# Sliding 8x8 windows with stride 4: the order of the band-crossing stores, the last units and five loads

## The chip, the core and the metric

The kernel runs on one core of one Trainium2 chip. Times are microseconds (us) of device time. The core has compute engines that copy data within the on-chip memory (DVE, the vector engine; ACT, the scalar engine; POOL, the general engine, which here only issues transfers), SP, which only issues transfers, and 16 DMA engines that move data between the device memory and the 128 partitions of the on-chip memory. "Row" below means 4096 floats, 16 KB, which lie together in one partition and together in the output.

## The reference

The input x has shape (16, 64, 64, 64): batch, channel, height, width, float32. Each 8x8 window at a stride of 4 is copied out, all channels together; there is no arithmetic.

```python
n_h = (h - window_size) // stride + 1      # 15
n_w = (w - window_size) // stride + 1      # 15
result = np.zeros((batch, n_h, n_w, c, window_size, window_size), dtype=np.float32)
for i in range(n_h):
    for j in range(n_w):
        h_start = i * stride
        w_start = j * stride
        result[:, i, j] = x[:, :, h_start:h_start + window_size, w_start:w_start + window_size].copy()
```

The input has 16.8 MB and the output 59.0 MB: 16 x 15 x 15 = 3600 rows.

## The kernel before, in words

**Layout.** The whole input is loaded once, into the tile L. A partition holds one channel half (ch, two halves of 32 channels), one batch (b, 16) and one horizontal band of 16 image rows (q, 4 bands): partition = ch * 64 + b * 4 + q. The batches come in two groups of eight, y = 0 and 1, so a group of one channel half takes 32 partitions.

**Loads (L56 to L58, L106 to L114).** ACT issues one load of 512 KB (L106: 8 channels of the upper channel half, band 0, all batches). Then, for each y and q, SP issues one load for channels 4 to 31 of channel half 0 (`SMALL` = 4; 896 KB), and POOL one of channels 0 to 3 of that half (128 KB) and one for channel half 1 (1024 KB, or 768 KB for q = 0). SP has eight loads, POOL sixteen. Every one of SP's and POOL's loads writes 8 partitions.

**Units.** A unit fills one of four buffers G (128 partitions x one row) by copies from L, and one store sends its rows out. `tile_()` (L169) hands out the buffers in turn; a buffer is free again when its earlier store has landed. A window at band slot s = 0, 1 or 2 (rows 0, 4, 8 of the band) lies inside a band; the one at slot 3 crosses into the next band, so its lower half comes from the next partition, through a stream shuffle (L151). The units are:

- `part(y, j)` (L174), six of them: one batch group, slots 0 and 1 and two columns j, j + 1; copies of 32 partitions on ACT and DVE (L181).
- `unit(j, 0)` (L189, a plain unit), eight of them, j = 6 to 13: slot 0 in partitions 0 to 63, slot 1 in 64 to 127. In each half `fill` (L139) makes one copy with the first of two copy functions (ACT, L148) and one with the second: `dve` for the three early ones, otherwise `shf` (a stream shuffle that moves nothing across, on DVE, L158) or `mix` (8 of 32 channels on ACT, L162, the others by `shf`).
- `unit(j, 2)` (a crossing unit), fifteen of them, j = 0 to 14: slot 2 in one half of the partitions, copied by ACT; slot 3 in the other, by `shf`, `mix` and the shuffles of L151. `turn` (L198), which alternates, says which half has slot 2. With turn 0 slot 2 lies in partitions 0 to 63 and slot 3 in 64 to 127, and the scatter uses the index tile `idx_hi`; with turn 1 it is the other way round, with `idx_lo`. Band 3 has no slot 3 (that would be window row 15 of 15), so the index of its 16 rows, those with q = 3 in the half that has slot 3, is set past the end of the output and they are not written.

POOL sends out these units by indirect scatters of 128 rows (L128), which know the output row of each partition from the index tile.

**Order.** It is the order of the code, written out by hand: three parts for y = 0; three parts for y = 1, each followed by a plain unit; then five times three crossing units and a plain unit. The 29 units use the buffers 0, 1, 2, 3, 0, ...; the last plain unit (j = 13) is the 29th.

**The last two units (L218 to L230).** Column j = 14 still lacks slots 0 and 1. One buffer is skipped (L219). Each of the two is filled in partitions 32 to 95 by four copies of 32 partitions (L227; for each y one on ACT for channel half 0 and one on DVE for channel half 1), and is stored by four transfers (L230), one for each band q, of 16 rows each (256 KB). The four of s = 0 are issued by SP; of s = 1, q = 0 and 2 by SP, 1 and 3 by ACT. At the end of the kernel SP waits for all transfers (shown under L261).

Of the kernel before, what the change touches and what calls it, by code (L numbers as in the profile page):

```python
# [10 lines left out]
def kernel(  # L11
# [7 lines left out]
    nc = tc.nc  # L19
    P = nc.NUM_PARTITIONS  # L20

    B, C, H, W = x.shape
    Bo, NH, NW, Co, WSo, WSo2 = out.shape
    WS = int(window_size)
    ST = int(stride)
# [5 lines left out]
    CH = 2  # L31
    HQ = P // (B * CH)
    CL = C // CH
    RB = H // HQ
    NSLOT = RB // ST
    NWIN = NH * NW
    CFREE = C * WS * WS
    HP = P // CH
    YB = 8
    NY = B // YB  # L40
    QP = YB * HQ
# [7 lines left out]
    L = lpool.tile([P, CL, RB, W], f32)  # L49
# [1 line left out]

    SMALL, HWP = 4, 8

    def load(eng, ch, y, q, c0, c1):  # L56
        p0 = ch * HP + y * QP + q
        eng.dma_start(out=L[p0 : p0 + QP - HQ + 1 : HQ, c0:c1, :, :], in_=x_v[ch, y, q, :, c0:c1, :])  # L58
# [49 lines left out]
    for y in range(NY):  # L108
        for q in range(HQ):
            hw = y * HQ + q < HWP  # L110
            if hw:
                load(nc.sync, 0, y, q, SMALL, CL)
            load(nc.gpsimd, 0, y, q, 0, SMALL if hw else CL)
            load(nc.gpsimd, 1, y, q, EC if q == 0 else 0, CL)  # L114

# [5 lines left out]
    o_q = out.rearrange("b i j c r w -> i j b (c r w)")  # L121

    def free(st):
        tc.declare_no_dep(st.ins, group="stores", reason="each store writes rows of its own")
        tc.add_to_no_dep_group("stores", st.ins)

    def scatter(g, ix, j, s):
        st = nc.gpsimd.indirect_dma_start(  # L128
            out=o_v,
            out_offset=bass.IndirectOffsetOnAxis(ap=ix[:, 0:1], axis=0),  # L130
            in_=g.rearrange("p c r w -> p (c r w)"),
            in_offset=None,
            element_offset=(s * NW + j) * CFREE,
            bounds_check=B * NWIN - 1,
            oob_is_err=False,
        )
        free(st)

    def fill(g, half, s, j, lo, n, copies):  # L139

        d = slice(half * HP + lo, half * HP + lo + n)
        cols = slice(j * ST, j * ST + WS)
        for ch in (half, 1 - half):
            f = slice(ch * HP + lo, ch * HP + lo + n)
            cs = slice(ch * CL, (ch + 1) * CL)
            copy = copies[ch != half]
            if s < NSLOT - 1:
                copy(out=g[d, cs, :, :], in_=L[f, :, s * ST : s * ST + WS, cols])  # L148
            else:
                copy(out=g[d, cs, 0:ST, :], in_=L[f, :, s * ST : RB, cols])  # L150
                nc.vector.stream_shuffle(out=g[d, cs, ST:WS, :], in_=L[f, :, 0:ST, cols], mask=nxt)  # L151

    act, dve = nc.scalar.copy, nc.vector.tensor_copy
# [3 lines left out]
    def shf(out, in_):  # L157
        nc.vector.stream_shuffle(out=out, in_=in_, mask=same)  # L158

    def mix(out, in_):  # L160
        k = out.shape[1] // 4
        act(out=out[:, 0:k], in_=in_[:, 0:k])  # L162
        shf(out=out[:, k:], in_=in_[:, k:])


    EARLY = 3
    at = 0

    def tile_():  # L169
        nonlocal at  # L170
        at += 1
        return G[(at - 1) % NG]

    def part(y, j):  # L174
        g = tile_()
        for d in range(P // QP):
            s, dj = d // NY, d % NY
            cols = slice((j + dj) * ST, (j + dj) * ST + WS)
            for ch in range(CH):
                f = (ch * NY + y) * QP  # L180
                (act if (2 * d + ch) % 3 == 0 else dve)(  # L181
                    out=g[d * QP : (d + 1) * QP, ch * CL : (ch + 1) * CL, :, :],
                    in_=L[f : f + QP, :, s * ST : s * ST + WS, cols],
                )
        scatter(g, (idx_y0, idx_y1)[y], j, 0)

    crossed = 0

    def unit(j, s, fast=False):  # L189
        nonlocal crossed  # L190
        g = tile_()
        if s == 0:
            fill(g, 0, 0, j, 0, HP, (act, dve if fast else shf))
            fill(g, 1, 1, j, 0, HP, (act, dve if fast else mix))
            scatter(g, idx, j, s)
        else:

            turn = crossed % 2  # L198
            crossed += 1
            fill(g, turn, s, j, 0, HP, (act, act))  # L200
            fill(g, 1 - turn, s + 1, j, 0, HP, (shf, mix))
            scatter(g, (idx_hi, idx_lo)[turn], j, s)

    for n in range(EARLY):
        part(0, 2 * n)
    plain = [(j, 0) for j in range(2 * EARLY, NW - 1)]
    cross = [(j, 2) for j in range(NW)]
    for n in range(EARLY):
        part(1, 2 * n)
        unit(*plain.pop(0), fast=True)  # L210
    while plain:
        for w in cross[:3]:
            unit(*w)
        cross = cross[3:]
        unit(*plain.pop(0))


    j = NW - 1  # L218
    tile_()  # L219
    for s in range(2):  # L220
        g = tile_()
        cols = slice(j * ST, j * ST + WS)
        for y in range(NY):
            d = slice(QP + y * QP, QP + (y + 1) * QP)
            for ch, copy in enumerate((act, dve)):
                f = slice(ch * HP + y * QP, ch * HP + (y + 1) * QP)
                copy(out=g[d, ch * CL : (ch + 1) * CL, :, :], in_=L[f, :, s * ST : s * ST + WS, cols])  # L227
        g_q = g.rearrange("p c r w -> p (c r w)")
        for q in range(HQ):
            free((nc.sync, nc.scalar)[s * q % 2].dma_start(out=o_q[q * NSLOT + s, j], in_=g_q[QP + q : QP + q + (B - 1) * HQ + 1 : HQ]))  # L230


# [33 lines left out]
```

## Time and profile before

| | |
|---|---|
| median of 3 runs | 190.38 us (190.26 to 190.56) |
| span of the profiled execution, from the first to the last instruction | 189.0 us |
| busy: DVE, ACT, POOL | 142.5, 139.2, 46.9 us |
| moved by the DMA engines | 75.81 MB, mean 401 GB/s |
| copies of a full 64-partition half on ACT (L148) | 46 of 1896 ns |

The span is what the profile measures of one execution; the time of a run is taken around the whole execution, and the two differ by 1.4 us. The profile gives no other time for its own execution.

How to read it: the windows give, for a stretch of time, its length, the busy time of DVE, ACT and POOL (with the number of instructions), the clock of the unused matrix engine, the mean busy share of the 16 DMA engines and what they moved. A packet is counted in the window in which it starts, so the share of a short window can be a little off, above 1.0 too. In the timeline a line has start, duration, engine, source line, operation, output<-input, count, and in brackets the idle time before it with what ended it. "POOLq", "SPq" and "ACTq" are the instruction queues of engines: the issue of transfers and waits on semaphores.

### The profile page before, as it was taken

What the parts mean: (1) busy time and instruction counts of PE and PEld (TensorE: products, weight loads), DVE (VectorE), ACT (ScalarE), POOL (GpSimd) and SP (SyncE); (2) the same over time, 40 slices, a digit from 0 to 9 for tenths busy, and PEclk for the clock granted to TensorE, in tenths of its full rate; (3) what the DMA queues carried; (4) which work ended last, traced back from release to release, by engine and by line L of the source; (5) the groups of instructions that cost most, each with busy time, mean ns of one, the idle gap of its engine ahead of it and who ended that gap; (6) DMA issues with size and microseconds to landing.
All of it is one profiled execution on the core that took longest, in us unless ns stands there. A gap on an engine that the chain in (4) does not pass through costs nothing.

```text
span 189.0 us, 557 instructions
## 1 busy us (share of the span) xinstructions
DVE 142.5 (75%) x200; ACT 139.2 (74%) x89; POOL 46.9 (25%) x50
## 2 busy tenths in 40 slices
DVE  4000009999697979799989999999999999997410
ACT  0000009998699999988889999999999999974740
POOL 7321212207217170522220222222222222223000
DMA  4999999999999999999999999999999999999993
GB/s 118 308 409 397 402 401 397 397 403 394 427 434 420 435 434 416 434 434 413 437 437 408 439 430 420 423 437 416 427 413 434 428 409 430 406 437 378 427 389 153
DMA packets 11044, 75.81 MB, mean 401 GB/s; under 512 B 3344, under 2 KB 3344, under 8 KB 7440
## 3 DMA queue, kind: packets, MB, share of 16 engines
q0 software_dynamic: 8784, 65.81, 84.0%
q1 hardware_dynamic: 2048, 8.91, 12.0%
q10 hardware_dynamic: 208, 1.05, 1.8%
q14 instruction: 4, 0.03, 0.0%
HBM read 16.78 MB, written 62.91 MB: 422 GB/s over the span
## 4 chain that ended last, share of the span: by engine, by line
DMA 66%; DVE 18%; issue 6%; ACT 3%; POOL 2%; DVEq 0%; ACTq 0%; PEldq 0%
DMA out_dram<-G,idx_hi 24%; DMA L<-in_x_dram 23%; DMA out_dram<-G,idx 13%; DVE G L158 10%; DMA out_dram<-G,idx_y 7%; DVE G L151 5%; DVE G L181 3%; ACT G L227 2%; POOL L L58 2%; ACT G L148 1%; DVE G L148 0%; DVEq L181 0%; POOL pi L69 0%; DVEq L158 0%; PEldq L261 0%
## 5 line engine op out<-in xcount | busy, mean ns | idle before, releaser
L148 ACT COPY G<-L 64x2048 f32<-64x2048 f32 x46 | 87.2, 1896 | 5.5 <-DMA out_dram<-G,idx 2.3
L181 DVE COPY G<-L 32x2048 f32<-32x2048 f32 x30 | 36.6, 1221 | 29.3 <-DMA L<-in_x_dram 26.7
L158 DVE STREAM_SHUFFLE G<-L 64x1024 f32<-64x1024 f32 (+3 forms) x40 | 55.7, 1392 | 1.3
L151 DVE STREAM_SHUFFLE G<-L 64x1024 f32<-64x1024 f32 x30 | 38.5, 1282 | 0.0
L181 ACT COPY G<-L 32x2048 f32<-32x2048 f32 x18 | 33.9, 1896 | 2.9 <-DMA L<-in_x_dram 2.3
L181 ACT ACT_TABLE_LOAD x1 | 1.3, 1283 | 28.3 <-DMA L<-in_x_dram 28.3
L58 POOL DMA_DIRECT2D L<-in_x_dram x16 | 10.9, 691 | 23.0 <-DMA L<-in_x_dram 22.5
L128 POOL DMA_INDIRECT out_dram<-G,idx_y x6 | 10.0, 1664 | 25.5 <-DVE G L181 24.5
L128 POOL DMA_INDIRECT out_dram<-G,idx x8 | 11.3, 1412 | 19.9 <-DVE G L158 6.5
L128 POOL DMA_INDIRECT out_dram<-G,idx_hi x8 | 7.7, 963 | 30.7 <-DVE G L151 23.1
L128 POOL DMA_INDIRECT out_dram<-G,idx_lo x7 | 6.7, 961 | 27.5 <-DVE G L151 19.1
L227 ACT COPY G<-L 32x2048 f32<-32x2048 f32 x4 | 7.6, 1896 | 5.1 <-DMA out_dram<-G,idx_lo 4.0
L162 ACT COPY G<-L 64x256 f32<-64x256 f32 (+1 forms) x20 | 9.1, 456 | 0.5
L227 DVE COPY G<-L 32x2048 f32<-32x2048 f32 x4 | 4.9, 1219 | 3.5 <-DMA out_dram<-G,idx_hi 2.4
L148 DVE COPY G<-L 64x2048 f32<-64x2048 f32 x6 | 7.3, 1222 | 0.2
L158 DVE LOAD_MASK_SELECT G<-L x40 | 0.4, 9 | 2.1 <-DMA out_dram<-G,idx_y 1.2
L72 DVE TENSOR_SCALAR tb<-pi 128x1 int32<-128x1 int32 x1 | 0.2, 153 | 1.0 <-POOL pi L69 1.0
L78 DVE TENSOR_TENSOR th<-tc,tq 128x1 int32<-128x1 int32 x2 | 0.3, 156 | 0.0
L75 DVE TENSOR_SCALAR th<-tc 128x1 int32<-128x1 int32 x2 | 0.3, 154 | 0.0
L69 POOL IOTA pi<- 128x1 int32 x1 | 0.1, 124 | 0.4 <-PEq L261 0.4
L151 DVE LOAD_MASK_SELECT G<-L x30 | 0.2, 7 | 0.0
L78 DVE CUSTOM_DVE_ANT_0 idx_lo<-tb,th 128x2 uint16<-128x2 uint16 x1 | 0.2, 159 | 0.0
(18 smaller groups left out, 2.6 us busy)
## 6 DMA issues: line engine op xcount, KB each, us to landing
L<-in_x_dram SPq DMA_DIRECT2D x8, 896.0 KB
L<-in_x_dram POOLq DMA_DIRECT2D x6, 1024.0 KB, 21.6
L<-in_x_dram POOLq DMA_DIRECT2D x2, 768.0 KB, 18.3
out_dram<-G SPq DMA_DIRECT2D x6, 256.0 KB
L<-in_x_dram POOLq DMA_DIRECT2D x8, 128.0 KB, 21.6
L<-in_x_dram ACTq DMA_DIRECT2D x1, 512.0 KB
out_dram<-G ACTq DMA_DIRECT2D x2, 256.0 KB
out_dram<-G,idx POOLq DMA_INDIRECT x8, 12.3
```

What stands on the lines that cost most here:

```text
L58: eng.dma_start(out=L[p0 : p0 + QP - HQ + 1 : HQ, c0:c1, :, :], in_=x_v[ch, y, q, :, c0:c1, :])
L69: nc.gpsimd.iota(pi[:, :], pattern=[[0, 1]], base=0, channel_multiplier=1)
L72: nc.vector.tensor_scalar(out=d[:, :], in0=pi[:, :], scalar1=shift, scalar2=mask, op0=ALU.logical_shift_right, op1=ALU.bitwise_and)
L75: nc.vector.tensor_scalar(out=d[:, :], in0=a[:, :], scalar1=float(m), scalar2=None, op0=ALU.mult)
L78: nc.vector.tensor_tensor(out=d[:, :], in0=a[:, :], in1=b[:, :], op=op)
L128: st = nc.gpsimd.indirect_dma_start(out=o_v, out_offset=bass.IndirectOffsetOnAxis(ap=ix[:, 0:1], axis=0), in_=g.rearrange("p c r w -> p (c ...
L148: copy(out=g[d, cs, :, :], in_=L[f, :, s * ST : s * ST + WS, cols])
L151: nc.vector.stream_shuffle(out=g[d, cs, ST:WS, :], in_=L[f, :, 0:ST, cols], mask=nxt)
L158: nc.vector.stream_shuffle(out=out, in_=in_, mask=same)
L162: act(out=out[:, 0:k], in_=in_[:, 0:k])
L181: (act if (2 * d + ch) % 3 == 0 else dve)(out=g[d * QP : (d + 1) * QP, ch * CL : (ch + 1) * CL, :, :], in_=L[f : f + QP, :, s * ST : s * S ...
L227: copy(out=g[d, ch * CL : (ch + 1) * CL, :, :], in_=L[f, :, s * ST : s * ST + WS, cols])
```

## The change

- Crossing units: `turn` begins with 1 instead of 0, so that the first is an `idx_lo` unit and every one is the other kind than before.
- The last plain unit (j = 13): the second copy of each half is split at channel 12, 12 channels on ACT and 20 by `shf` in one half, 12 on ACT and 20 by a DVE copy in the other. (Before: `shf` of 32 channels, and `mix`.) The other units keep their copy functions.
- The last two units (j = 14, s = 0 and 1): no buffer is skipped; each of the four 32-partition copies is split at channel 12 between ACT and DVE, so eight copies for each unit; and the unit is stored by one transfer of 64 rows (1 MB), issued by SP, instead of four of 16.
- Loads: SP's loads of (y, q) = (0, 0) to (0, 3) and (1, 0) are each split into two of 14 channels (4 to 17 and 18 to 31; 448 KB each).

```diff
-    SMALL, HWP = 4, 8
+    SMALL, HWP, TWICE = 4, 8, 5
...
             if hw:
-                load(nc.sync, 0, y, q, SMALL, CL)
+                mid = (SMALL + CL) // 2 if y * HQ + q < TWICE else CL
+                load(nc.sync, 0, y, q, SMALL, mid)
+                if mid < CL:
+                    load(nc.sync, 0, y, q, mid, CL)
             load(nc.gpsimd, 0, y, q, 0, SMALL if hw else CL)
...
-    def mix(out, in_):
-        k = out.shape[1] // 4
-        act(out=out[:, 0:k], in_=in_[:, 0:k])
-        shf(out=out[:, k:], in_=in_[:, k:])
+    def split(k, other):
+        def both(out, in_):
+            act(out=out[:, 0:k], in_=in_[:, 0:k])
+            other(out=out[:, k:], in_=in_[:, k:])
+
+        return both
+
+    mix = split(CL // 4, shf)
...
+    ACT_C = 12
...
-    def unit(j, s, fast=False):
+    def unit(j, s, copies=(shf, mix)):
...
-            fill(g, 0, 0, j, 0, HP, (act, dve if fast else shf))
-            fill(g, 1, 1, j, 0, HP, (act, dve if fast else mix))
+            fill(g, 0, 0, j, 0, HP, (act, copies[0]))
+            fill(g, 1, 1, j, 0, HP, (act, copies[1]))
...
-            turn = crossed % 2
+            turn = 1 - crossed % 2
...
-        unit(*plain.pop(0), fast=True)
+        unit(*plain.pop(0), (dve, dve))
...
-        unit(*plain.pop(0))
+        unit(*plain.pop(0), *([] if len(plain) else [(split(ACT_C, shf), split(ACT_C, dve))]))
...
+    o_e = out.rearrange("b i j c r w -> j b i (c r w)")
     j = NW - 1
-    tile_()
     for s in range(2):
...
-            for ch, copy in enumerate((act, dve)):
+            for ch in range(CH):
                 f = slice(ch * HP + y * QP, ch * HP + (y + 1) * QP)
-                copy(out=g[d, ch * CL : (ch + 1) * CL, :, :], in_=L[f, :, s * ST : s * ST + WS, cols])
+                for c0, c1, copy in ((0, ACT_C, act), (ACT_C, CL, dve)):
+                    copy(out=g[d, ch * CL + c0 : ch * CL + c1, :, :], in_=L[f, c0:c1, s * ST : s * ST + WS, cols])
         g_q = g.rearrange("p c r w -> p (c r w)")
-        for q in range(HQ):
-            free((nc.sync, nc.scalar)[s * q % 2].dma_start(out=o_q[q * NSLOT + s, j], in_=g_q[QP + q : QP + q + (B - 1) * HQ + 1 : HQ]))
+        free(nc.sync.dma_start(out=o_e[j, :, s : s + (HQ - 1) * NSLOT + 1 : NSLOT], in_=g_q[QP : QP + HP]))
```

## Prediction

> **What bounds the kernel now.** I read the page first, then busy time in chosen windows, then the timeline around the last stores.
>
> ```profile
> span 189.0 us, 557 instructions
> DVE 142.5 (75%) x200; ACT 139.2 (74%) x89; POOL 46.9 (25%) x50
> DMA packets 11044, 75.81 MB, mean 401 GB/s; under 512 B 3344, under 2 KB 3344, under 8 KB 7440
> HBM read 16.78 MB, written 62.91 MB: 422 GB/s over the span
> ```
>
> The span is 189.0 us; the median of the shown runs, 190.38, is 1.4 us more, and I carry that 1.4 unchanged. No compute engine is above 75%. The two byte counts differ: 16.78 + 62.91 = 79.69 MB asked for, 75.81 MB moved. The missing 3.88 MB is, at 16,384 bytes a row, 237 rows: nearly the 15 x 16 = 240 rows that the fifteen crossing scatters push out of bounds. An out-of-bounds row is not moved.
>
> The windows (duration, busy time of DVE, ACT and POOL, clock, share of the 16 DMA engines, GB/s):
>
> ```profile
> 0.00:2.00 2.00, 0.91 (x9) 0.00 (x0) 0.84 (x6) 1.00 0.00 0
> 2.00:5.00 3.00, 1.43 (x11) 0.00 (x0) 3.00 (x6) 1.00 0.83 198
> 20.00:25.00 5.00, 0.00 (x0) 0.00 (x0) 1.21 (x2) 1.00 1.04 398
> 85.00:95.00 10.00, 9.52 (x15) 8.59 (x7) 1.93 (x2) 1.00 1.00 424
> 145.00:155.00 10.00, 9.89 (x15) 9.23 (x7) 2.85 (x3) 1.00 1.01 422
> 174.20:175.00 0.80, 0.80 (x1) 0.78 (x2) 0.00 (x0) 1.00 0.54 225
> 181.00:185.60 4.60, 0.00 (x0) 0.41 (x1) 0.00 (x0) 1.00 0.91 381
> 185.60:186.40 0.80, 0.00 (x0) 0.00 (x0) 0.00 (x0) 1.00 0.54 225
> 186.00:187.00 1.00, 0.00 (x0) 0.00 (x0) 0.00 (x0) 1.00 0.28 115
> ```
>
> From 5 us to 174 us the transfers are saturated: 1.04 while loading, 1.00 while storing. That is the bound. The telling rows are the two with 0.54 and 225 GB/s: about half of 424, so **eight of the sixteen engines are idle** and eight still work. At 174.2 that is a pause; from 185.6 it is the end: eight engines are done, the others work until about 187.0 (115 KB, seven rows, start after 186.0).
>
> Why halves? Landings answer. These rows begin where a copy got its buffer back, that is, where a store had landed:
>
> ```profile
> 146.78 3.82 ACT L148 COPY G<-L 64x2048 f32<-64x2048 f32 x2 [0.66 <-DMA out_dram<-G,idx]
> 155.72 3.82 ACT L148 COPY G<-L 64x2048 f32<-64x2048 f32 x2 [0.24 <-DMA out_dram<-G,idx_hi]
> 172.70 3.81 ACT L227 COPY G<-L 32x2048 f32<-32x2048 f32 x2 [3.99 <-DMA out_dram<-G,idx_lo]
> 177.59 3.81 ACT L227 COPY G<-L 32x2048 f32<-32x2048 f32 x2 [1.07 <-DMA out_dram<-G,idx_hi]
> ```
>
> The last idx_hi store lands 177.59 - 172.70 = 4.89 us after the idx_lo store before it. An engine at 424 / 16 = 26.5 GB/s moves 4.89 x 26.5 / 16.4 = 7.9 rows in that time: the eight of a full 128-row store, though this one moves only 112. Between 146.78 and 155.72 lie one idx_lo and one idx_hi: 8.94 us, which leaves 4.05 for the idx_lo, six to seven rows. So the half that lands last carries 8 rows of an idx_hi store and 6 of an idx_lo store. idx_hi drops the q = 3 rows of the upper 64 partitions; the lagging half is thus the one that carries the **lower 64 partitions**, and the other, with six rows of the idx_hi store, is the one idle at 174.2. Before has eight idx_hi and seven idx_lo stores. The lower half has no visible pause, because the other half always runs dry first; its row count sets the end.
>
> **The swapped turns.** Eight idx_hi and seven idx_lo become seven and eight. The lower half moves two rows fewer, the upper two more. A row is 4.89 / 8 = 0.61 us, so the lower half ends 1.22 us earlier, if it is always fed. Instructions, copies and shuffles of a crossing unit stay the same; only the partition halves change roles.
>
> The upper half now ends at 185.6 + 1.22 = 186.8 if its pauses stay, and that would be the new end. Its pauses: 0.8 x 0.46 x 2 = 0.74 us at 174.2, and 4.6 x 0.09 x 2 = 0.83 us in the last stores. If both go, it ends at about 185.3, before the lower half's 187.0 - 1.22 = 185.8.
>
> **The last units, and the dropped tile_().** What feeds that pause:
>
> ```profile
> 158.66 0.96 POOL L128 DMA_INDIRECT out_dram<-G,idx_hi  x1 [3.77 <-DVE G L151]
> 164.26 3.82 ACT L148 COPY G<-L 64x2048 f32<-64x2048 f32 x2
> 167.44 2.42 DVE L158 STREAM_SHUFFLE G<-L 64x2048 f32<-64x2048 f32 x1
> 168.10 0.62 ACT L162 COPY G<-L 64x512 f32<-64x512 f32 x1
> 168.17 0.96 POOL L128 DMA_INDIRECT out_dram<-G,idx_hi  x1 [3.80 <-ACT G L148]
> 169.90 1.85 DVE L158 STREAM_SHUFFLE G<-L 64x1536 f32<-64x1536 f32 x1
> 172.51 1.58 POOL L128 DMA_INDIRECT out_dram<-G,idx  x1 [3.38 <-issue]
> 176.54 7.58 SPq L230 DMA_DIRECT2D out_dram<-G  x6
> 181.44 2.19 ACTq L230 DMA_DIRECT2D out_dram<-G  x2
> ```
>
> The last plain unit (j = 13) ends on DVE at 171.75, three us after ACT; its scatter goes out at 172.51. The new pieces have 12 channels (768 elements a partition) on ACT and 20 (1280) on DVE. Their neighbours:
>
> ```profile
> L148 ACT COPY G<-L 64x2048 f32<-64x2048 f32 x46 | 87.2, 1896 | 5.5 <-DMA out_dram<-G,idx 2.3 <-DMA out_dram<-G,idx_hi 1.3 <-DMA out_dram<-G,idx_y 0.8
> L158 DVE STREAM_SHUFFLE G<-L 64x1024 f32<-64x1024 f32 x15 | 19.2, 1283 | 0.5
> L227 DVE COPY G<-L 32x2048 f32<-32x2048 f32 x4 | 4.9, 1219 | 3.5 <-DMA out_dram<-G,idx_hi 2.4 <-DMA out_dram<-G,idx_lo 1.0
> L158 DVE STREAM_SHUFFLE G<-L 64x1536 f32<-64x1536 f32 x5 | 9.3, 1861 | 0.2
> L162 ACT COPY G<-L 64x512 f32<-64x512 f32 x5 | 3.1, 617 | 0.1
> ```
>
> ACT at 768: 0.62 + 256 x (1.896 - 0.617) / 1536 = 0.83 us. Shuffle at 1280: halfway between 1.28 and 1.86, 1.57. DVE copy at 1280: between 0.76 (in proportion) and 1.22 (no saving); I take 0.82. The last plain unit then costs ACT 2 x 1.90 + 2 x 0.83 = 5.5 us from 164.26, to 169.8, and DVE 1.57 + 0.82 with a gap, 2.5 us from 167.44, to 170.0. Its scatter goes out at about 170.7 instead of 172.51, 1.8 us earlier; the pause at 174.2 lasts 0.8, so it is covered. With the swap the last crossing store also occupies the upper half two rows longer, which covers it by itself.
>
> Final unit s = 0: without the skipped tile it takes the buffer of the store three before the last plain one (issued 158.66), landed about 4.05 before 172.65, at 168.6: no wait. ACT 4 x 0.83 and DVE 4 x 0.82 run side by side, to about 173.3. Unit s = 1 takes the buffer landing at 172.65, again no wait, and is filled at about 176.8. Before, their stores began at 176.54 and 181.44. At 176.8 the lower half still has eight rows of the j = 13 store and four of s = 0, over 7 us of work, so neither half runs dry at the end. The 1.8 and 4.6 us gained here are worth nothing by themselves on the lower half; they only remove the upper half's pauses.
>
> **One transfer for each final store.** Eight transfers of 256 KB become two of 1 MB. The trace has no 64-row store. Neighbours and load rows:
>
> ```profile
> L230 SPq DMA_DIRECT2D out_dram<-G x6: 592/1343/1388, 176.5 to 182.9; - x6
> L106 ACTq DMA_DIRECT2D L<-in_x_dram x1: 686/686/686, 0.7 to 0.7; - x1
> L58 SPq DMA_DIRECT2D L<-in_x_dram x8: 677/3202/6515, 0.7 to 21.4; - x8
> 1.48 4.99 POOL L58 DMA_DIRECT2D L<-in_x_dram  x8 [0.52 <-issue]
> 9.36 0.55 POOL L58 DMA_DIRECT2D L<-in_x_dram  x1 [2.89 <-DMA L<-in_x_dram]
> ```
>
> Issue lies between 0.6 and 6.5 us; I take 1.4, the nearest row. Even 6.5 for s = 0, from 173.4 to 179.9, puts s = 1 out before the queue is empty at 183. So: nothing, if 64 rows spread over 16 engines, four each, as 4 x 16 rows did. The Trainium skill, "DMA: Bandwidth & Descriptors", section "Why a DMA increments its semaphore by 16 and not by 1", says that the engines used are the largest number up to 16 that divides the outermost size on both sides; here 64 and 16, so 16, and it speaks for this choice. No run here shows a 64-row store yet.
>
> It changes the last waits too. SP ends with a chain of waits:
>
> ```profile
> SPq L261 <- DMA out_dram<-G: 3.4, 1, 3.4
> L261 SPq EVENT_SEMAPHORE  x8: 27/28/28, 187.6 to 188.1; - x8
> ```
>
> Eight waits in 0.5 us, of which the first ended the 3.4 us wait at 187.6: the last store's semaphore is asked first, seven waits follow at about 0.063, 0.44 us. POOL's ninth load waited for a landing after eight went out freely, so I read eight semaphores handed out in turn. Before has 9 + 8 = 17 transfers from SP and ACT, and the seventeenth has the first semaphore; after has 14 + 2 = 16, and the last has the eighth. The seven waits are then over before it lands. I take 0.44; the bounds are 0 and 0.44.
>
> **Five loads split.** Thirteen loads on SP instead of eight; those past the eighth SP/ACT transfer wait for a landing eight transfers earlier. Behind them on SP are only later loads; seven transfers of 448 KB or more, over 3 MB, stay queued, and SP's issue was already held back (3.2 us median). Bytes and engines are the same. I take 0. Below nothing: an earlier first packet could win part of the 0.17 x 3 = 0.5 us missing at 2 to 5 us. Above: the rival below. A rule of the Trainium skill speaks against splitting: "DMA: Bandwidth & Descriptors", section "Anatomy of one DMA — SWDGE (gpsimd) path", gives each DMA a fixed part of about 2.0 us, and its "Rules for kernel authors" ask for 1 MiB or more; by that, five more loads cost 10 us where nothing overlaps them, and the sum would be 198.7, as an estimate from that page. The row at 20 to 25 us, where POOL's 128 KB loads (4 channels of 8 partitions) run among the others with the engines at 1.04, speaks for overlap.
>
> **Sum**: 189.0 - 1.22 - 0.44 = 187.3; plus 1.4, **188.7 us**.
>
> **Rivals.**
> - *The upper half ends last* because its pauses at 174 to 185 stay: 186.8 against 187.0, minus 0.44: 190.38 - 0.2 - 0.44 = 189.7. For it: DVE is busy 9.9 of 10 us, so supply is close to its limit. Against: the scatter has 1.8 us in hand. 12%.
> - *No gain*: a half is held by something not seen (buffers, issue), and the saved rows turn into a pause: 190.4. 5%.
> - *The other way round, slower*: if the end-setting half is that of the upper partitions, the swap gives it two rows more: 190.38 + 1.22 - 0.44 = 191.2. It decides if the half idle at 174.2 is not the half done at 185.6. The 4.89 us landing of an idx_hi store speaks against. 6%.
> - *The 1 MB store does not spread*: on eight engines each would carry 16 final rows instead of 8, 4.9 us more on the lagging half: 193.6. 4%.
> - *Split loads pay a latency each*: first bytes come after 2.0 us, issue was at 0.74, so 1.3 us or more each: 188.7 + 6.5 = 195.2. 3%.
>
> The forecast, with its partial forms from 188.2 (the half us at the start) to 189.15 (no gain in the last waits), has 68%; 2% are left for what I do not see, on the slow side. The range 188.2 to 189.9 holds forecast and first rival, 80%. A measurement of this kernel tells about 0.2%, 0.4 us, from no change: faster 0.82 (with a little of the third case), same 0.04, slower 0.14.
>
> **What would show it.** Right: the window at 174 no longer drops to half; idx_lo appears eight times; the last data packets start 1.2 us earlier in both halves, within about 0.5 us of each other; the final SP waits do not follow the landing; final stores are issued near 173 and 177. Wrong: a share of half for over 1 us near the end, an ACT or DVE wait for a store in the last units, share below 1.0 during loads.

## The result, and the profile after

The changed kernel takes 188.90 us (median of 4 runs, 188.61 to 189.08), the kernel before 190.41 beside it: ratio 0.9915, 95% interval 0.9897 to 0.9933. It is faster by 0.9%. The forecast was 188.7. The profiled execution took 189.08 us, the slowest of the four, with a span of 187.3; that this is the span of the forecast is chance (see below).

The page of the kernel after, the lines that answer to those of before:

```profile
span 187.3 us, 567 instructions
DVE 142.5 (76%) x203; ACT 139.3 (74%) x94; POOL 45.0 (24%) x50
DMA packets 10988, 75.81 MB, mean 405 GB/s; under 512 B 3288, under 2 KB 3288, under 8 KB 7384
L131 POOL DMA_INDIRECT out_dram<-G,idx_lo x8 | 7.7, 961 | 30.6 <-DVE G L154 26.9
```

The same bytes and the same compute time in a shorter span; the mean rate, 405 instead of 401 GB/s, is only the bytes divided by the span. There are eight `idx_lo` stores now instead of seven. Where the time went, the windows of the kernel after show:

```profile
2.00:5.00 3.00, 1.43 (x11) 0.00 (x0) 3.00 (x6) 1.00 0.85 213
85.00:95.00 10.00, 9.65 (x15) 8.73 (x7) 2.07 (x3) 1.00 1.01 431
174.20:175.00 0.80, 0.79 (x2) 0.79 (x2) 0.00 (x0) 1.00 0.92 389
178.00:182.00 4.00, 0.00 (x0) 0.00 (x0) 0.00 (x0) 1.00 1.00 426
184.00:185.00 1.00, 0.00 (x0) 0.00 (x0) 0.00 (x0) 1.00 0.77 328
185.20:186.00 0.80, 0.00 (x0) 0.00 (x0) 0.00 (x0) 1.00 0.05 20
```

At 174.2 the share is 0.92 instead of 0.54. At the end there is no stretch at half any more: nearly all engines finish shortly after 185. After 185.2 one row is still started (20 GB/s for 0.8 us is 16 KB), which one engine moves; that engine sets the end of the data. Before, eight engines were still at work until about 187.0.

The last units in the timeline of the kernel after, and the two groups of copies of the last two units:

```profile
168.25 0.96 POOL L131 DMA_INDIRECT out_dram<-G,idx_lo  x1 [3.77 <-DVE G L154]
168.98 0.88 DVE L166 COPY G<-L 64x1280 f32<-64x1280 f32 x1
169.15 0.83 ACT L165 COPY G<-L 64x768 f32<-64x768 f32 x1
170.63 1.04 POOL L131 DMA_INDIRECT out_dram<-G,idx  x1 [1.42 <-ACT G L165]
173.39 3.98 SPq L238 DMA_DIRECT2D out_dram<-G  x2
```

```profile
L236 ACT COPY G<-L 32x768 f32<-32x768 f32 x8 | 6.6, 830 | 0.1
L236 DVE COPY G<-L 32x1280 f32<-32x1280 f32 x8 | 6.5, 818 | 0.1
```

The last scatter goes out at 170.63 (170.7 was forecast), the final stores are issued at 173.39 and 176.8 (173.4 and 176.8), and the new pieces take 830 and 818 ns (0.83 and 0.82 us).

The end of SP's work, from its waits (who waited for whom, us in total, times, longest) and the waits of L269 between 186 and 187 us:

```profile
SPq L269 <- DMA out_dram<-G: 1.5, 1, 1.5
L269 SPq EVENT_SEMAPHORE  x2: 17/22/28, 186.4 to 186.7; - x2
```

One wait starts as the last store lands, at 186.4; the other, at 186.7, is already the common end of all engines. Before, eight in a row stood there, from 187.6 to 188.1.

### The profile page after: what moved, and what is told of

It is laid out like the page before. It is cut to its first block, busy times and chain, and to the rows that moved or that the text cites. A ratio compares the mean times of both kernels' runs of the same rounds, so it can differ in the third digit from the quotient of the medians.

```text
span 187.3 us, 567 instructions
## 1 busy us (share of the span) xinstructions
DVE 142.5 (76%) x203; ACT 139.3 (74%) x94; POOL 45.0 (24%) x50
## 4 chain that ended last, share of the span: by engine, by line
DMA 53%; DVE 28%; issue 6%; ACT 5%; POOL 2%; ACTq 1%; DVEq 0%; PEldq 0%
DMA L<-in_x_dram 20%; DMA out_dram<-G,idx_y 14%; DVE G L161 14%; DMA out_dram<-G,idx 13%; DVE G L154 9%; DMA out_dram<-G,idx_lo 6%; DVE G L189 4%; ACT G L236 3%; POOL L L58 2%; ACT G L151 1%; ACT G L165 1%; ACTq L269 1%; DVE G L151 0%; POOL pi L69 0%; DVEq L161 0%
## 5 line engine op out<-in xcount | busy, mean ns | idle before, releaser
L189 DVE COPY G<-L 32x2048 f32<-32x2048 f32 x30 | 36.7, 1224 | 29.9 <-DMA L<-in_x_dram 24.1
L161 DVE STREAM_SHUFFLE G<-L 64x1024 f32<-64x1024 f32 (+4 forms) x39 | 53.0, 1360 | 1.3
L189 ACT COPY G<-L 32x2048 f32<-32x2048 f32 x18 | 33.9, 1896 | 4.1 <-DMA L<-in_x_dram 2.8
L131 POOL DMA_INDIRECT out_dram<-G,idx_lo x8 | 7.7, 961 | 30.6 <-DVE G L154 26.9
L131 POOL DMA_INDIRECT out_dram<-G,idx x8 | 9.2, 1152 | 17.8 <-DVE G L161 6.8
L131 POOL DMA_INDIRECT out_dram<-G,idx_hi x7 | 6.7, 960 | 27.0 <-DVE G L154 19.0
L165 ACT COPY G<-L 64x256 f32<-64x256 f32 (+2 forms) x21 | 10.2, 484 | 0.5
L236 ACT COPY G<-L 32x768 f32<-32x768 f32 x8 | 6.6, 830 | 0.1
L236 DVE COPY G<-L 32x1280 f32<-32x1280 f32 x8 | 6.5, 818 | 0.1
L166 DVE COPY G<-L 64x1280 f32<-64x1280 f32 x1 | 0.9, 876 | 0.0
```

Of the source, the lines that this page charges most:

```text
L131: st = nc.gpsimd.indirect_dma_start(out=o_v, out_offset=bass.IndirectOffsetOnAxis(ap=ix[:, 0:1], axis=0), in_=g.rearrange("p c r w -> p (c ...
L166: other(out=out[:, k:], in_=in_[:, k:])
L189: (act if (2 * d + ch) % 3 == 0 else dve)(out=g[d * QP : (d + 1) * QP, ch * CL : (ch + 1) * CL, :, :], in_=L[f : f + QP, :, s * ST : s * S ...
L236: copy(out=g[d, ch * CL + c0 : ch * CL + c1, :, :], in_=L[f, c0:c1, s * ST : s * ST + WS, cols])
```

## The experiments

Medians in us; "kernel before" is 190.41 to 190.57 in the different sets of runs, and the ratio is against the one of its own set.

| run | edit | median | ratio to before, 95% |
|---|---|---|---|
| changed kernel | | 188.90 | 0.9915 (0.9897 to 0.9933) |
| e1 | before, swap alone | 189.58 | 0.9959 (0.9946 to 0.9972) |
| e2 | changed, without the swap | 190.24 | 0.9982 (0.9968 to 0.9996) |
| e3 | changed, no load split | 189.41 | 0.9940 (0.9927 to 0.9953) |
| e4 | changed, last units filled as before | 188.81 | 0.9912 (0.9900 to 0.9925) |
| e5 | e4 without the swap | 189.82 | 0.9963 (0.9950 to 0.9977) |
| e6 | changed, six loads split | 189.38 | 0.9943 (0.9929 to 0.9956) |
| e7 | changed, one more idx_lo unit | 189.03 | 0.9922 (0.9908 to 0.9935) |
| e8 | e4, first ACT load of 5 channels | 189.06 | 0.9927 (0.9913 to 0.9941) |
| e9 | before, one more idx_hi unit | 191.75 | 1.0072 (1.0052 to 1.0093) |
| e10 | e4, one more idx_lo, ACT load of 12 channels | 189.46 | 0.9943 (0.9928 to 0.9957) |
| e11 | e4, one more idx_lo, ACT load of 10 channels | 188.83 | 0.9912 (0.9898 to 0.9927) |

**The swap: e1, e2, e9, e7.** The theory counts rows on the late half of the engines; the rivals put the gain elsewhere.

```diff
 e1, on the kernel before
-            turn = crossed % 2
+            turn = 1 - crossed % 2
```

> The kernel before with the turns of the crossing units swapped, nothing else. Theory (the half of the engines that carries the lower 64 partitions sets the end, and loses two rows of 0.61 us): that half ends 1.2 us earlier; the other half, which has two rows more, fills its own pause at 174 us with them and ends at about 186.0, so 189.2 to 189.5 us; the final waits keep their order (the last store's semaphore is asked first). Rival A (the swap pays only together with the new last units, since the other half keeps its pauses): 190.2. Rival B (the swap has no part in the gain): 190.4.

189.58: 0.85 us faster than the kernel before in its set, 190.43 (0.53 to 1.03 by the interval), so the swap pays without anything else, and rivals A and B fall. The window at the pause, in e1:

```profile
174.20:175.00 0.80, 0.80 (x1) 0.78 (x2) 0.00 (x0) 1.00 1.16 471
```

The pause of half the engines is gone though the last scatter is not earlier: the upper half fills it with its two additional rows.

```diff
 e2, on the changed kernel
-            turn = 1 - crossed % 2
+            turn = crossed % 2
```

> The changed kernel with the turns as they were before. Theory: the lower half has its two rows back, so data end 1.2 us later than in the changed kernel; only the order of the final waits (0.44 us) is left of the gain: 190.0 us. Rival B (last units, single stores and split loads carry the gain): 188.9 to 189.2.

190.24: nearly all of the gain goes, and rival B falls. It is 0.24 more than the theory said, and the twelve runs spread from 189.54 to 190.67, more widely than those of any other experiment; e5 takes that up. The end of the data is at half again, two us long:

```profile
184.00:185.00 1.00, 0.00 (x0) 0.00 (x0) 0.00 (x0) 1.00 0.47 197
185.00:186.00 1.00, 0.00 (x0) 0.00 (x0) 0.00 (x0) 1.00 0.46 197
```

The next run goes the other way from the kernel before.

```diff
 e9, on the kernel before
-            turn = crossed % 2
+            turn = 0 if crossed > 12 else crossed % 2
```

> The kernel before with one more crossing unit turned the other way (j = 13): nine idx_hi and six idx_lo stores, nothing else. Theory (a linear price: each idx_lo turned to idx_hi gives the late half two rows, 1.2 us): 190.43 + 1.2 = 191.65 us. Rival (the swap gained by the order of the stores, or by which of them is last, not by the count of rows): 190.4, since the last store stays an idx_hi store.

191.75, 0.7% above the kernel before in its set (190.57): 1.0 to 1.8 us for two rows more on each engine of the lower half, though the last crossing store is an idx_hi store as before. The edit also puts three idx_hi stores in a row; the next run puts three idx_lo stores in a row and loses nothing measurable by it. So the price is in the count of rows.

```diff
 e7, on the changed kernel
-            turn = 1 - crossed % 2
+            turn = 1 if crossed > 12 else 1 - crossed % 2
```

> The changed kernel with one more crossing unit turned (j = 13): nine idx_lo and six idx_hi stores. Theory (the end is set by the half with more rows plus loads; after the change both halves end their data at about 185.1 but for one engine of the lower half at 186.0): the upper half gets two rows more and ends at 186.3, so no gain: 189.1 us, 0.2 more than the changed kernel. Rival (every idx_hi turned to idx_lo gains 1.2 us): 187.7.

189.03: no further gain. The same edit that was worth about 1 us from eight to seven idx_hi stores is worth nothing from seven to six, because the other half is now the late one. (The profile does not name the engines; which half is late is known from the count of rows.) The end of its data, again at half:

```profile
184.00:185.00 1.00, 0.00 (x0) 0.00 (x0) 0.00 (x0) 1.00 0.46 197
185.00:186.00 1.00, 0.00 (x0) 0.00 (x0) 0.00 (x0) 1.00 0.31 131
```

**The last waits and the split loads: e3, e6.** Both change how many transfers SP and ACT issue, and so which of eight semaphores the last store has.

```diff
 e3 and e6, on the changed kernel
-    SMALL, HWP, TWICE = 4, 8, 5
+    SMALL, HWP, TWICE = 4, 8, 0      # e3
+    SMALL, HWP, TWICE = 4, 8, 6      # e6
```

> The changed kernel with no load split (eight loads on SP as before). Theory (the split matters only through the turn of the eight semaphores: now 9 + 2 = 11 transfers, the last store has the third, and five waits follow its landing): 188.9 + 0.3 = 189.2 us, with the data ending at the same time. Rival (split loads feed the engines earlier): 189.2 or more too, but with data ending later; rival (split loads cost something): below 188.9.

> The changed kernel with six loads split instead of five: 15 + 2 = 17 transfers from SP and ACT, so the last store has the first of the eight semaphores again and seven waits follow its landing. Theory: 188.9 + 0.44 = 189.3 us though the loads are cut finer. Rival (splitting loads itself is what helps or costs nothing): 188.9 or less.

189.41 and 189.38: both about 0.5 us above the changed kernel. With six loads split, which cuts the loads finer, all eight waits stand behind the landing of the last store again (waits of L269 between 184.5 and 186.5 us, e6):

```profile
L269 SPq EVENT_SEMAPHORE  x8: 27/28/28, 186.0 to 186.4; - x8
```

In e6 it is therefore the order of the waits, not the loads: five splits make 16 transfers, and 16 is a multiple of eight. For e3 the theory gave 0.3 and 0.5 was measured. Its trace shows the 0.3: the last store lands at 186.4 as in the changed kernel, five more waits follow the one that ends there (waits between 186 and 187 us), and the span is 187.6 instead of 187.3.

```profile
L269 SPq EVENT_SEMAPHORE  x6: 28/28/28, 186.4 to 186.7; - x6
```

The other 0.2 is within the intervals. Earlier loading by the splits does not show: from 2 to 5 us the engines' share is 0.93 in e3 and 0.85 in the changed kernel, and the kernel before and e1, whose loads are the same, differ by as much (0.83 and 0.94).

**The fills of the last units: e4, e5.**

```diff
 e4, on the changed kernel
-        unit(*plain.pop(0), *([] if len(plain) else [(split(ACT_C, shf), split(ACT_C, dve))]))
+        unit(*plain.pop(0))
...
+    tile_()
     for s in range(2):
...
-            for ch in range(CH):
+            for ch, copy in enumerate((act, dve)):
                 f = slice(ch * HP + y * QP, ch * HP + (y + 1) * QP)
-                for c0, c1, copy in ((0, ACT_C, act), (ACT_C, CL, dve)):
-                    copy(out=g[d, ch * CL + c0 : ch * CL + c1, :, :], in_=L[f, c0:c1, s * ST : s * ST + WS, cols])
+                copy(out=g[d, ch * CL : (ch + 1) * CL, :, :], in_=L[f, :, s * ST : s * ST + WS, cols])
```

> Swap, split loads and single final stores as in the changed kernel, but the last plain unit and the last two units are filled as before (whole copies, one buffer skipped). Theory (swap and order of the final waits carry all; the fills only had to be in time, and final stores issued at about 176.5 and 181.4 still find both halves busy until 183): 188.9 us, at most 0.2 more. Rival A (the earlier fills are needed because the half with two rows more runs dry): 189.4 or more, with a share of about half for some tenths of a us near 174 or 183.

188.81: the new fills are worth nothing that can be measured, and the skipped buffer costs nothing. The swap, with the order of waits that single stores and five splits give, carries nearly all; what the parts come to is added up below. Nor does a half run dry:

```profile
174.20:175.00 0.80, 0.80 (x1) 0.78 (x2) 0.00 (x0) 1.00 1.10 451
```

```diff
 e5, on e4
-            turn = 1 - crossed % 2
+            turn = crossed % 2
```

> The run with the old fills (split loads, single final stores), but with the turns as before the change as well: only split loads and single stores are left of it. It differs from the run without the swap by the late fills alone. Theory (POOL's final drain ends 1.9 us after the last scatter has landed; early final stores share the engines with that scatter and push its landing back, to 185.8 us in the run without the swap, where the drain, at 187.7, was later than the last store): with late final stores the last scatter lands before 184 and the drain is out of the way, so 190.43 - 0.44 = 190.0 us, below the 190.24 of the run without the swap. Rival (the drain costs nothing, 190.24 is the two rows and the waits): 190.2 to 190.3.

189.82 against 190.24 in e2: later fills are, if anything, better here. The scatter of the last plain unit and POOL's final drain, first e2, then e5:

```profile
L131 POOL DMA_INDIRECT out_dram<-G,idx x1: 1031/1031/1031, 170.6 to 170.6; - x1
DMA to landing us min/median/max: 15.2/15.2/15.2
L269 POOLq DRAIN  x3: 51/105/17346, 170.4 to 188.2; - x3
SPq L269 <- PEq L269: 1.2, 2, 0.7
```

```profile
L131 POOL DMA_INDIRECT out_dram<-G,idx x1: 1422/1422/1422, 172.7 to 172.7; - x1
DMA to landing us min/median/max: 10.9/10.9/10.9
L269 POOLq DRAIN  x3: 51/105/13007, 172.5 to 187.9; - x3
SPq L269 <- PEq L269: 0.7, 2, 0.5
```

In e2 the scatter starts at 170.6 and lands 15.2 us later, at 185.8; the drain that starts at 170.4 ends 17.3 us later, at 187.7. In e5 the scatter is issued 2.1 us later and lands 2.2 us earlier, at 183.6; the drain ends at 185.5. In both the drain ends 1.9 us after the landing. What delays the scatter in e2 are the final stores, which go out at 173.2 and 176.6 there and at 176.6 and 181.5 in e5. From 176.5 to 181 us the share of the 16 engines that went to queue q1, which carries SP's transfers, was (first e2, then e5):

```profile
q1 hardware_dynamic: 50, 0.82, 42.8%
```

```profile
q1 hardware_dynamic: 17, 0.28, 14.6%
```

POOL's scatters, on queue q0, had the rest. In e2 the drain holds the end: SP, done with its own waits, waits 1.2 us in total for the other engines at the common end, against 0.7 in e5, where the drain is out of the way. The profiles show it plainly, 0.5 us in one execution of each; the intervals of the two runs (0.9968 to 0.9996 and 0.9950 to 0.9977) overlap a little.

In the e5 window at the pause half the engines stand idle again, and in e4, which differs by the swap alone, they do not:

```profile
174.20:175.00 0.80, 0.80 (x1) 0.78 (x2) 0.00 (x0) 1.00 0.54 225
```

**Moving loads between the halves: e8, e10, e11.** The theory, carried on, says that bytes can be moved between the halves in the loads as well, in finer steps: ACT's load uses all 16 engines, what it leaves falls to POOL's loads on the upper half.

```diff
 e8, e10 and e11, on e4
-    EC = 8
+    EC = 5      # e8;  12 in e10, 10 in e11
...
-            turn = 1 - crossed % 2
+            turn = 1 if crossed == 1 else 1 - crossed % 2      # e10 and e11
```

> The run with the old fills, with ACT's first load of 5 channels instead of 8 (EC = 5), so that 3 packets of 4 KB per engine of the lower half move to the loads of the upper half: at 398 GB/s, 0.165 us each, the lower half ends 0.49 us earlier, the upper 0.49 later (185.1 to 185.6), and the one late engine of the lower half ends at about 185.5: 188.81 - 0.4 = 188.4 us. Rival A (ACT's load covers the time until SP's first packets, and a shorter one leaves the lower half idle at 3 to 4 us): 188.8. Rival B (the halves do not set the end): 188.8 as well, but with unchanged last packets.

189.06, no gain: rival A. Rival B falls, since the end did change: from 185.2 to 186 us the engines' share is 0.20 in e8 and 0.00 in e4. The windows of 3 to 5 us, first e4, then e8:

```profile
3.00:4.00 1.00, 0.55 (x4) 0.00 (x0) 1.00 (x2) 1.00 0.93 229
4.00:5.00 1.00, 0.00 (x0) 0.00 (x0) 1.00 (x3) 1.00 0.91 213
```

```profile
3.00:4.00 1.00, 0.54 (x4) 0.00 (x0) 1.00 (x2) 1.00 0.72 168
4.00:5.00 1.00, 0.00 (x0) 0.00 (x0) 1.00 (x3) 1.00 0.67 180
```

0.21 + 0.24 = 0.45 us of all engines is lost in these two us, while ACT's load is over and SP's loads are only beginning. If it all falls on one half, that is 0.9 us, more than the 0.49 that the move of three packets was to bring it. (Over these two us e8's share is 0.70; in the eleven other kernels profiled it is 0.92 to 1.06.)

> The run with the old fills, with one more crossing unit turned (j = 1: nine idx_lo and six idx_hi) and ACT's first load of 12 channels instead of 8. Theory (halves are to end together, and the upper half stands idle at 4.5 to 6 us until POOL's first loads arrive): the lower half has 4 packets of 4 KB more and two rows less, 0.66 - 1.22 = 0.56 us earlier; the upper has 4 packets less and two rows more, and works in 0.6 us of its idle time, so it ends where it did: 188.81 - 0.5 = 188.3 us. Rival (the idle time of the upper half at the start stays, it only moves): the upper half ends 0.6 us later, 188.9 to 189.1.

> The same with 10 channels in ACT's load: lower half 0.33 - 1.22 = 0.9 us earlier, upper half -0.33 + 1.22 less 0.33 of idle time at the start, 0.55 us later: 188.8 us, the upper half last.

e11 came out at 188.83 as expected, e10 at 189.46: the theory's 188.3 was wrong. The start is full in e10 (the first row), but about half of the engines stand idle just before the first scatter is there (the second; the third is the same stretch in e4). By the theory these are the engines of the upper half, which now has done its loads:

```profile
4.00:6.00 2.00, 0.00 (x0) 0.00 (x0) 2.00 (x5) 1.00 1.04 205
44.00:45.00 1.00, 0.97 (x2) 1.00 (x2) 0.61 (x1) 1.00 0.56 221
```

```profile
44.00:45.00 1.00, 0.99 (x2) 1.00 (x1) 0.83 (x1) 1.00 1.11 442
```

The first scatter also goes out 0.84 us later in e10 than in e4 (first e10, then e4); why it does was not tried.

```profile
43.22 1.40 POOL L131 DMA_INDIRECT out_dram<-G,idx_y  x1 [9.71 <-ACT G L189]
```

```profile
42.38 1.38 POOL L131 DMA_INDIRECT out_dram<-G,idx_y  x1 [8.50 <-DVE G L189]
```

Idle time at the start was exchanged for idle time before the first scatter: nearer to the rival than to the theory. No version tried beats the changed kernel by more than its intervals; e4 is as fast with the simpler code.

## Why the prediction was right, point by point

- **The sum, 1.66 us of gain.** 1.51 was measured (1.3 to 2.0 by the interval), and the mechanism holds. That the number came so close is in part luck. From the kernel before to e1, the swap alone, 0.85 was gained, and from e1 to e4 another 0.77: the swap brought 0.37 less than the 1.22 forecast and the rest 0.33 more than the 0.44, and the two misses cancel. The traces account for about 0.4 of the 0.77 by the waits; the rest is near the width of the intervals and unexplained.
- **The 1.4 us between span and time.** Wrong. In every run for which both are on record, of both kernels and of all experiments, the time is 1.8 us above the span (189.08 and 187.3; 190.41 and 188.6). The prediction took the span from one execution and the time from others: the one with 189.0 must have taken about 190.8, more than the 190.26 to 190.56 of the three runs shown. The forecast time hangs on the median 190.38 and is not touched by this; the forecast span is. The median run went from a span of about 188.6 to about 187.1, and the 187.3 was met because both profiles are of executions longer than the median.
- **The swap, 1.22 us.** Right in mechanism and sign, and in place (the late half, rows of the lower partitions). Its size, undone and redone: 0.85 (e1), 1.0 (e4 to e5), 1.2 (e9 against its set), and 1.3 from the changed kernel to e2, which holds about 0.5 of POOL's drain. Without that last one, 1.22 is the upper end: it supposes that all engines of the late half are equally late. In the kernel after one engine still runs after 185.2, and such a one may cut short what the time shows; why it is late was not tried.
- **The order of the last waits, 0.44 us.** Right. From the landing of the last store to the end of the span the traces show 1.4 us before and 1.3 in e6, with seven waits in it, 1.2 in e3 with five, and 0.9 in the changed kernel with none. The times agree: e6 is 0.48 above the changed kernel, though the two intervals (0.9929 to 0.9956 and 0.9897 to 0.9933) overlap a little. It was read from a count of transfers, 17 against 16. The rule of eight semaphores in turn is confirmed by e6 and e3, both on the side of more time.
- **Single final stores, nothing.** Right as far as the runs tell: e3, which has them without split loads, is 0.17 below e1, and two waits fewer behind the landing are 0.13 of it. SP's issue took 0.66 and 0.60 us, less than the 1.4 taken. The stores spread over all engines. e4 shows it best: its scatters have landed by 181.2 and its first final store by 183.7, so that only the second is left from 183.8 to 184.4, and it takes 0.96 of the engines' time (the line below). That is what the Trainium skill ("DMA: Bandwidth & Descriptors", section "Why a DMA increments its semaphore by 16 and not by 1") says for outermost sizes of 64 and 16, and the trace agrees; the rival of eight engines is out.

```profile
183.80:184.40 0.60, 0.00 (x0) 0.00 (x0) 0.00 (x0) 1.00 0.96 410
```

- **The last units.** The durations and times were right within 0.1 us, and "worth nothing by themselves on the lower half" too. But the prediction let the first rival (the upper half ends last) hang on the pauses that these fills were to remove. e1 and e4 show that the swap fills that pause itself; the sentence that said so should have lowered that rival's 12%. Unforeseen was a cost: early final stores push back the last scatter, in the kernel after to a landing 13.9 us after its issue (9.1 in e4), and POOL's drain, from 170.4 for 16.0 us, ends at 186.4, just as the last store lands, so that here it costs next to nothing. The prediction forgot that POOL too waits at the end.

```profile
L269 POOLq DRAIN  x3: 51/105/16036, 170.4 to 187.0; - x3
```

- **Split loads, nothing in the loading.** Right as far as the runs tell: one more split costs the 0.48 of the waits and no more (e6), against the fixed 2.0 us for each transfer that the same page of the Trainium skill gives in "Anatomy of one DMA — SWDGE (gpsimd) path". That section is about transfers issued by POOL; these are SP's, and others run beside them. Which of the two keeps the cost from showing was not tried.
- **The other way round, and no gain.** The result, e1 and e9 exclude both. With e7 they show the end moving as the count of rows and loads on each half says.
- **One sign did not fit the prediction's own sum.** It asked for last packets 1.2 us earlier in both halves, while its sum had the upper half end at 185.6 before and about 185.3 after. The trace bears out the sum: from 185.2 to 186 us the share of the engines is 0.05, so the half that was done at 185.6 before gained only some tenths of a us.

## What to carry to other kernels

When a kernel is bound by transfers, the mean rate hides which engines move them: a window whose share stays near a half at the end, or an idle half beside a full one, is work to be moved from one half to the other, and the price is one row's time for each row. Moving it pays until the other half is late, no further. And look at what the kernel waits for after the last byte: a count of transfers, or a scatter issued shortly before the last stores, can be worth half a microsecond.

## What the runs showed that was not expected

- POOL's drain at the end of the kernel ends 1.9 us after the landing of its last scatter (e2: 185.8 and 187.7; e5: 183.6 and 185.5).
- Issuing the final stores earlier lets them share the engines with the scatter before them, which then lands later: 15.2 us after issue instead of 10.9 (e2, e5).
